# Making the low part of every fourth weight chunk with ScalarE and an adding DMA instead of VectorE

## The chip, the cores and the metric

The kernel runs on one core of one Trainium2 chip. The metric is the device time of one execution in microseconds (us). PE is TensorE, DVE is VectorE, ACT is ScalarE, POOL is GpSimd and SP is SyncE, whose queue issues most transfers.

## The reference, cut to what matters

Two layers work on 512 rows of width 2048. Each one norms its rows, projects them, mixes them, projects again and adds the normed result to its input:

```python
def even_mixer(h, w_in, pool_w, pool_scale, w_out, cos, sin):
    z = h @ w_in
    a_in, a_gate, q, k, v, b_gate = jnp.split(z, _split_points(EVEN_COLS), axis=-1)
    ya = causal_pool_mixer(a_in, pool_w, pool_scale) * jax.nn.silu(a_gate)
    yb = dilated_attention(q, k, v, cos, sin) * jax.nn.silu(b_gate)
    return jnp.concatenate([ya, yb], axis=-1) @ w_out
...
    for i in range(DEPTH):
        if i % 2 == 0:
            h = rmsnorm(x, e_pre_norm[j])
            y = even_mixer(h, e_w_in[j], e_pool_w[j], e_pool_scale[j], e_w_out[j], cos, sin)
            x = x + rmsnorm(y, e_post_norm[j])
        else:
            h = rmsnorm(x, o_pre_norm[j])
            y = odd_mixer(h, o_w_in[j], o_sgu_norm_g[j], o_sgu_norm_b[j], o_sgu_w[j], o_sgu_b[j],
                          o_conv_w[j], o_conv_b[j], o_conv_norm_g[j], o_conv_norm_b[j], o_w_out[j])
            x = x + rmsnorm(y, o_post_norm[j])
```

The odd layer's mixer has the same two projections around a gating unit and a convolution of width 31. All data are float32.

## The kernel before, in words

All large weights are cut into 402 chunks of 128 x 1024 float32 (512 KB), which are used in one fixed order, numbered 0 to 401. A float32 product is made of three products of a narrower type (float32r): weight and activation are both split into a high part (the value rounded) and a low part (the rest), and PE adds low x high, high x low and high x high. The activations' parts stand in the buffers `Ah` and `Al`. The weights' parts are made while the program runs, by `Weights.split`: SP loads the raw chunk into a `wraw` buffer (L54), ACT writes the rounded copy `whi` (L64), and DVE subtracts it from the raw chunk to give `wlo` (L65). There are three buffers each for `wraw`, `whi` and `wlo`, so the parts of chunk i go where those of chunk i-3 were, and ACT can start on chunk i when PE has ended chunk i-3. A raw buffer is free for its next load when both the parts have been made from it.

PE uses a chunk in one of two ways. `zt_item` (L137 to L139) and `nat_item` with four row tiles (L162 to L164) issue 24 matmuls on each chunk; stages of these are called full-width here. `nat_item` with two row tiles issues 12 on each chunk; these are columns 2 and 3 of each output projection (`out_projection`, 32 chunks in each layer) and the odd layer's `owv` projection (32 chunks). They are called half-width stages here: chunks 210 to 273 and 370 to 401, 96 chunks. In a half-width stage the matmuls on one chunk begin with one or two that take `whi` (L162), and the first that takes `wlo` (L163) comes right after them.

The instructions' order on each engine is set at build time by a scheduler, which estimates times of its own; each engine then runs its own list in that order, and waits on semaphores. POOL does little: small scalar steps of the norms (`rsqrt_of`, L114 and L116), the reductions over partitions of the attention and the convolution, and some stores. At the end of each half of an output projection, `boundary` adds the normed rows to x, stores them with a DMA issued by POOL (L328) and has PE transpose them (L222).

Of the kernel before, what the change touches and what calls it, by code (L numbers as in the profile page):

```python
# [13 lines left out]
F32 = mybir.dt.float32  # L14
FR = mybir.dt.float32r
AF = mybir.ActivationFunctionType
OP = mybir.AluOpType
# [18 lines left out]


class Weights:
    """Streams the weight chunks in the order of use and splits each into two float32r parts."""

    def __init__(self, nc, raw_pool, split_pool, chunks, raw_bufs, ahead):
        self.nc, self.raw_pool, self.split_pool, self.chunks = nc, raw_pool, split_pool, chunks
# [14 lines left out]
    def split(self, upto):  # L57
        while len(self.parts) < min(upto, len(self.chunks)):
            i = len(self.parts)
            self.load(i + 1)  # L60
            hi = self.split_pool.tile([P, 1024], FR, tag="whi", name=f"whi{i}")
            lo = self.split_pool.tile([P, 1024], FR, tag="wlo", name=f"wlo{i}")
            for c in ((slice(0, 512), slice(512, 1024)) if i == 0 else (slice(0, 1024),)):
                self.nc.scalar.activation(hi[:, c], self.raw[i][:, c], AF.Copy)  # L64
                self.nc.vector.tensor_tensor(lo[:, c], self.raw[i][:, c], hi[:, c].bitcast(F32), op=OP.subtract)  # L65
            self.parts.append((hi, lo))

# [9 lines left out]
def trunk(ctx: ExitStack, tc: tile.TileContext, x, xt, out, ewv, ewz, ewo, epw, epost,  # L77
# [38 lines left out]
        nc.gpsimd.tensor_tensor(r, v, neghalf, op=OP.pow)  # L116
        return r

# [1 line left out]
    items = []  # L120

    def add_item(chunks, pe, after=None):
# [88 lines left out]
        items.clear()  # L211
        return pos

# [1 line left out]
    def to_A(half, pcol0):  # L215
        rows = [yrow(2 * half), yrow(2 * half + 1)]
        for kq in range(8):
            ps = sbank(f"tr{half}_{kq}").rearrange("p (k t) -> p k t", k=2)
            for j in range(2):
                k = 2 * kq + j  # L220
                for t in range(2):
                    nc.tensor.transpose(ps[:, j, P * t:P * t + P], rows[t][:, P * k:P * k + P], ident)  # L222
            for j in range(2):
                k = 2 * kq + j
                g = pc[:, pcol0 + k:pcol0 + k + 1]
                ah = Ah[:, k, 256 * half:256 * half + 256]
                nc.scalar.activation(ah, ps[:, j, :], AF.Copy, scale=g)
                nc.vector.scalar_tensor_tensor(Al[:, k, 256 * half:256 * half + 256], ps[:, j, :], g,
                                               ah.bitcast(F32), op0=OP.mult, op1=OP.subtract)
            if kq % 2 == 1:  # L230
                yield 1

    post = {}

# [1 line left out]
    first = {}  # L236

    def first_loads(i, t, chunk):
# [94 lines left out]
            yield 1  # L333
        yield from to_A(half, P_OPRE)

# [1 line left out]
    def split_y(ks):  # L337
        for k in ks:
            nc.scalar.activation(Ah[:, k, :], Y[:, k, :], AF.Copy)
            nc.vector.tensor_tensor(Al[:, k, :], Y[:, k, :], Ah[:, k, :].bitcast(F32), op=OP.subtract)  # L340
# [37 lines left out]
                nat_item(wo, c, [2 * half, 2 * half + 1], evac(c), order=order,  # L378
                         stagger=layer == 1 and half == 1 and c == 3)

    # ================= start =================
    nc.gpsimd.memset(neghalf, -0.5)
    cones = cpool.tile([P, 1], F32, name="cones")
    nc.gpsimd.memset(cones, 1.0)
# [2 lines left out]
    for key in ("ssq", "v", "r"):  # L387
        first[key] = small.tile([P, 4], F32, name=f"first_{key}", bufs=1)

    # ================= even layer, attention =================  # L390
    att_stack = ExitStack()
    att = att_stack.enter_context(tc.tile_pool(name="att", bufs=1))
    V1 = att.tile([P, 4, S], F32, name="V1")
# [120 lines left out]
    chunk_list = []  # L514
    w = Weights(nc, raw_pool, split_pool, chunk_list, 3, 2)

    # The whole program's chunks are listed first, so that loads and splits run ahead of their use.
    program = []

    def section(build):  # L520
# [18 lines left out]

    section(build_attention)  # L540

    # ================= even layer, pooling =================
    mix = {}

    pooled = {}
# [66 lines left out]
    section(build_pooling)  # L612
    section(lambda: out_projection(ewo, 0, (4, 5, 6, 7, 0, 1, 2, 3)))

    # ================= odd layer =================
    od = {}

    def ov_after(c):
# [144 lines left out]
    section(build_odd)  # L763
    section(lambda: out_projection(owo, 1, range(8)))

    # ================= emission =================
    w.first_loads = first_loads
    w.load(3)
    start(norm_first())
# [111 lines left out]
def build(arrays):  # L881
    nc = bacc.Bacc("TRN2", target_bir_lowering=False, num_devices=1)
    args = {}
    for name, a in arrays.items():
        args[name] = nc.dram_tensor(f"in_{name}_dram", a.shape, mybir.dt.from_np(a.dtype), kind="ExternalInput").ap()
    args["out"] = nc.dram_tensor("out_0_dram", (S, D), F32, kind="ExternalOutput").ap()
    with tile.TileContext(nc, schedule_with_timeline_sim=True) as tc:
        trunk(tc, **args)
    return nc
# [7 lines left out]
```

## Time and profile before

| | |
|---|---|
| median of the timed runs | 2072.81 us (2 runs, 2072.59 to 2073.03) |
| profiled execution, span from first to last instruction | 2071.4 us |
| busy: PE / DVE / ACT / POOL | 2055.5 / 1156.7 / 647.1 / 87.4 us |
| mean granted TensorE clock | 0.999 |

The span is 1.4 us under the median of the timed runs. Busy time is the time in which an engine had an instruction in work; matmuls are pipelined, so two of them may overlap in the rows, and their starts tell more than their ends. "Idle before" of an instruction is the time in which its engine had nothing in work ahead of it, with what ended that time behind the arrow.

### The profile page before, as it was taken

To read this page: it belongs to the slowest core of one execution; us is meant where nothing else is said; L and a number is where in the kernel's file an instruction comes from. 1 tells how busy PE (TensorE), PEld (TensorE's weight loads), DVE (VectorE), ACT (ScalarE), POOL (GpSimd) and SP (SyncE) were. 2 spreads that over 40 slices of the span, in tenths; PEclk is the share of its full clock that TensorE was granted. 3 is DMA by queue.
4 is the path that set the end of the run, shared out by engine and by line. 5 is a ranking of instruction groups with operands and counts; after the bars stand their busy time and mean duration, and the time that the engine had idled before them with its cause. 6 is when DMAs were issued, how large, how long until landed. Compare 5 with 4: busy or idle time off the path is not lost.

```text
span 2071.4 us, 22339 instructions
## 1 busy us (share of the span) xinstructions
PE 2055.5 (99%) x9064; PEld 1699.7 (82%) x9064; DVE 1156.7 (56%) x1385; ACT 647.1 (31%) x793; POOL 87.4 (4%) x86
## 2 busy tenths in 40 slices
PE   8999999999999999999999999999999999999998
PEld 8988888889988888888888888888888888888886
DVE  4725656555224656566542435775889996324255
ACT  6422222323222322223332324553122223323243
POOL 1000101000000101001000000100000001000002
PEclk9999999999999999999999999999999999999999
DMA  8332222232322222222223337864222222223465
GB/s 299 92 101 89 94 83 82 86 98 82 92 92 92 89 85 91 82 92 82 92 93 101 112 97 222 281 216 155 87 92 92 97 97 92 92 91 122 133 211 196
DMA packets 68472, 241.78 MB, mean 117 GB/s; under 512 B 7792, under 2 KB 8048, under 8 KB 67088
## 3 DMA queue, kind: packets, MB, share of 16 engines
q1 hardware_dynamic: 67152, 234.05, 35.0%
q0 software_dynamic: 1216, 6.29, 0.8%
q8 instruction: 71, 1.16, 0.2%
q14 instruction: 33, 0.27, 0.0%
HBM read 231.93 MB, written 8.39 MB: 116 GB/s over the span
## 4 chain that ended last, share of the span: by engine, by line
PE 97%; DMA 1%; DVE 1%; ACT 0%; issue 0%; POOL 0%; SPq 0%; DVEq 0%; ACTq 0%; POOLq 0%
PE z L138 20%; PE z L137 20%; PE z L139 20%; PE n L162 11%; PE n L163 11%; PE n L164 11%; PE sg L457 1%; DMA wraw<-in_owv_dram 0%; DVE Y L313 0%; PE ob L497 0%; PE ob L496 0%; PE oa L490 0%; PE sgu L640 0%; PE sa L445 0%; PE tr L222 0%; DMA wraw<-in_owo_dram 0%
## 5 line engine op out<-in xcount | busy, mean ns | idle before, releaser
L65 DVE TENSOR_TENSOR wlo<-wraw,whi 128x1024 fp32r<-128x1024 f32 (+1 forms) x403 | 504.1, 1251 | 571.3 <-ACT whi L64 570.6
L137 PE MATMUL z<-Ah,wlo 128*128 128x512 f32 x1792 | 710.5, 396 | 0.0
L138 PE MATMUL z<-Al,whi 128*128 128x512 f32 x1792 | 708.8, 396 | 0.0
L64 ACT ACTIVATE whi<-wraw 128x1024 fp32r<-128x1024 f32 (+1 forms) x403 | 425.5, 1056 | 906.9 <-PE z L139 463.8
L139 PE MATMUL z<-Ah,whi 128*128 128x512 f32 x1792 | 708.7, 395 | 0.0
L163 PE MATMUL n<-wlo,Ah 128*128 128x512 f32 x1024 | 406.8, 397 | 0.3 <-DVE wlo L65 0.2
L164 PE MATMUL n<-whi,Ah 128*128 128x512 f32 x1024 | 405.5, 397 | 0.0
L139 PEld LDWEIGHTS z<-Ah,whi 128*128 128x128 f32 x1792 | 336.6, 188 | 81.0
L137 PEld LDWEIGHTS z<-Ah,wlo 128*128 128x128 f32 x1792 | 336.7, 188 | 80.6
L138 PEld LDWEIGHTS z<-Al,whi 128*128 128x128 f32 x1792 | 336.7, 188 | 80.6
L162 PE MATMUL n<-whi,Al 128*128 128x512 f32 x1024 | 392.3, 398 | 6.7 <-DVE Al L263 6.7
L162 PEld LDWEIGHTS n<-whi,Al 128*128 128x128 f32 x1024 | 223.2, 218 | 41.6 <-DVE Al L263 6.7
L163 PEld LDWEIGHTS n<-wlo,Ah 128*128 128x128 f32 x1024 | 223.4, 218 | 36.3 <-DVE wlo L65 1.3
L164 PEld LDWEIGHTS n<-whi,Ah 128*128 128x128 f32 x1024 | 223.3, 218 | 35.0
L681 DVE SCALAR_TENSOR_TENSOR Y<-dp,pc,Y 128x512 f32<-128x512 f32 x240 | 174.3, 749 | 3.6
L423 DVE LOAD_MASK_SELECT sw<-qk x32 | 0.4, 14 | 125.4 <-ACT qk L422 125.4
L422 ACT ACTIVATE qk<-z 128x512 f32<-128x512 f32 x32 | 19.1, 597 | 145.3 <-PE z L139 145.3
L474 POOL PARTITION_ALL_REDUCE mw<-mv x8 | 14.3, 1784 | 798.9 <-DVE mv L472 798.9
L424 DVE TENSOR_TENSOR sw<-sw,rp 32x512 f32<-32x512 f32 x32 | 34.3, 1071 | 1.1
L425 DVE TENSOR_TENSOR qk<-qk,rp 32x512 f32<-32x512 f32 x32 | 34.0, 1063 | 0.0
L426 DVE TENSOR_TENSOR qk<-qk,sw 32x512 f32<-32x512 f32 x48 | 32.3, 673 | 0.2
L735 DVE TENSOR_TENSOR Y<-Y,og 128x512 f32<-128x512 f32 x16 | 11.1, 691 | 38.0 <-ACT og L734 38.0
(153 smaller groups left out, 908.1 us busy)
## 6 DMA issues: line engine op xcount, KB each, us to landing
wraw<-in_ewz_dram SPq DMA_DIRECT2D x144, 512.0 KB, 3.7
wraw<-in_owz_dram SPq DMA_DIRECT2D x80, 512.0 KB, 3.8
wraw<-in_ewo_dram SPq DMA_DIRECT2D x48, 512.0 KB, 4.2
wraw<-in_owo_dram SPq DMA_DIRECT2D x48, 512.0 KB, 3.9
wraw<-in_ewv_dram SPq DMA_DIRECT2D x47, 512.0 KB, 3.6
wraw<-in_owv_dram SPq DMA_DIRECT2D x32, 512.0 KB, 3.8
xn<-in_x_dram SPq DMA_DIRECT2D x4, 1024.0 KB, 8.7
xr<-in_x_dram SPq DMA_DIRECT2D x16, 256.0 KB, 5.1
```

Of the source, the lines that this page charges most:

```text
L64: self.nc.scalar.activation(hi[:, c], self.raw[i][:, c], AF.Copy)
L65: self.nc.vector.tensor_tensor(lo[:, c], self.raw[i][:, c], hi[:, c].bitcast(F32), op=OP.subtract)
L137: nc.tensor.matmul(ps, wl[:, j], Ah[:, k, :], start=first, stop=False)
L138: nc.tensor.matmul(ps, wh[:, j], Al[:, k, :], start=False, stop=False)
L139: nc.tensor.matmul(ps, wh[:, j], Ah[:, k, :], start=False, stop=last)
L162: nc.tensor.matmul(ps, tok(Al, k, t), wh[:, j], start=first, stop=False)
L163: nc.tensor.matmul(ps, tok(Ah, k, t), wl[:, j], start=False, stop=False)
L164: state["mm"] = nc.tensor.matmul(ps, tok(Ah, k, t), wh[:, j], start=False, stop=last).ins
L424: nc.vector.tensor_tensor(perm_out(sw), perm_out(sw), perm_in(sin), op=OP.mult)
L425: nc.vector.tensor_tensor(perm_out(t[0:32, :]), perm_out(t[0:32, :]), perm_in(cos), op=OP.mult)
L426: nc.vector.tensor_tensor(t[0:32, :], t[0:32, :], sw, op=OP.add)
L681: nc.vector.scalar_tensor_tensor(acc, dp[:, k:k + S], wk, acc, op0=OP.mult, op1=OP.add)
```

## The change

From chunk 16 on, every chunk whose number leaves 3 when divided by 4 (19, 23, ..., 399: 96 chunks) gets its low part in another way. ACT writes the rounded copy `whi` as before, and a second time the same copy with its sign turned into `wlo`. Then a DMA issued by POOL adds the raw chunk onto `wlo` where it stands. DVE has no part in these chunks. Of the 96, 24 lie in half-width stages (211, 215, ..., 271 and 371, 375, ..., 399). Behind L66 the lines of the changed kernel are numbered higher by 4, and `wlo` is negated in L66 and added to in L67. Comments that the change also takes out do nothing.

```diff
             for c in ((slice(0, 512), slice(512, 1024)) if i == 0 else (slice(0, 1024),)):
                 self.nc.scalar.activation(hi[:, c], self.raw[i][:, c], AF.Copy)
+                if i >= 16 and i % 4 == 3:
+                    self.nc.scalar.activation(lo, self.raw[i], AF.Copy, scale=-1.0)
+                    self.nc.gpsimd.dma_start(lo.bitcast(F32), self.raw[i], accum_op=OP.add)
+                    continue
                 self.nc.vector.tensor_tensor(lo[:, c], self.raw[i][:, c], hi[:, c].bitcast(F32), op=OP.subtract)
```

The scheduler orders the lists anew. In the rows below the number behind `whi`, `wlo` and `wraw` is that of the chunk; what follows the next underscore only tells buffers apart. On ACT, around chunk 219 in the first half-width stage (`junk0` is the squaring of an output column), the order before is

```order
L64 ACTIVATE whi217_7835<-wraw217_7781 128x1024
L64 ACTIVATE whi218_7854<-wraw218_7800 128x1024
L64 ACTIVATE whi219_7873<-wraw219_7820 128x1024
L64 ACTIVATE whi220_7895<-wraw220_7839 128x1024
L349 ACTIVATE junk0_6022,sq0_0_98<-n_210_0_7743 128x512
```

and in the changed kernel, at the same place of the same engine:

```order
L64 ACTIVATE whi217_7885<-wraw217_7830 128x1024
L64 ACTIVATE whi218_7904<-wraw218_7850 128x1024
L66 ACTIVATE wlo219_7924<-wraw219_7870 128x1024
L64 ACTIVATE whi219_7923<-wraw219_7870 128x1024
L353 ACTIVATE junk0_6058,sq0_0_98<-n_210_0_7792 128x512
L64 ACTIVATE whi220_7946<-wraw220_7889 128x1024
```

The negated copy comes ahead of the high part, so that the DMA's input is made first. At chunk 235 it is the other way round:

```order
L64 ACTIVATE whi235_8339<-wraw235_8268 128x1024
L66 ACTIVATE wlo235_8340<-wraw235_8268 128x1024
```

On POOL, the first boundary of the even layer has these rows before (`x1d` is the store of a row tile, `v_z` and `r_z` the scale of the next norm):

```order
L328 DMA x1d_85<-xr0_0_7735 128x2048
L114 TENSOR_SCALAR v_z0_8061<-ssz0_8059 128x1
L116 TENSOR_TENSOR r_z0_8063<-v_z0_8061,neghalf_84 128x1
L328 DMA x1d_85<-xr0_1_7814 128x2048
L114 TENSOR_SCALAR v_z1_8092<-ssz1_8090 128x1
L116 TENSOR_TENSOR r_z1_8094<-v_z1_8092,neghalf_84 128x1
```

and in the changed kernel these, up to the second boundary, with the adding DMAs (L67) among them:

```order
L332 DMA x1d_85<-xr0_1_7864 128x2048
L67 DMA wlo231_8226<-wraw231_8125 128x1024
L118 TENSOR_SCALAR v_z1_8145<-ssz1_8143 128x1
L120 TENSOR_TENSOR r_z1_8147<-v_z1_8145,neghalf_84 128x1
L67 DMA wlo235_8340<-wraw235_8268 128x1024
...
L332 DMA x1d_85<-xr0_3_8262 128x2048
L118 TENSOR_SCALAR v_z3_8578<-ssz3_8576 128x1
L120 TENSOR_TENSOR r_z3_8580<-v_z3_8578,neghalf_84 128x1
L67 DMA wlo247_8656<-wraw247_8558 128x1024
```

Chunk 231's DMA stands behind the store of a row tile, and chunk 247's behind the last step of the second boundary.

## Rows read from the trace of the kernel before

**Rows 1.** The page: busy time of the engines, and the chain that ended last.

```profile
PE 2055.5 (99%) x9064; PEld 1699.7 (82%) x9064; DVE 1156.7 (56%) x1385; ACT 647.1 (31%) x793; POOL 87.4 (4%) x86
...
PE 97%; DMA 1%; DVE 1%; ACT 0%; issue 0%; POOL 0%; SPq 0%; DVEq 0%; ACTq 0%; POOLq 0%
```

**Rows 2.** Waits of PE in the span: us in total, times, longest.

```profile
PE n L162 <- DVE Al L263: 6.7, 1, 6.7
PE n L163 <- DVE wlo L65: 0.2, 1, 0.2
```

**Rows 3.** The page's groups: busy, mean ns of one, idle before.

```profile
L65 DVE TENSOR_TENSOR wlo<-wraw,whi 128x1024 fp32r<-128x1024 f32 (+1 forms) x403 | 504.1, 1251 | 571.3 <-ACT whi L64 570.6
...
L64 ACT ACTIVATE whi<-wraw 128x1024 fp32r<-128x1024 f32 (+1 forms) x403 | 425.5, 1056 | 906.9 <-PE z L139 463.8
```

**Rows 4.** Timeline, full-width stage: chunk 28's last matmul, chunk 31's high part and first matmul.

```profile
171.52 0.40 PE L139 MATMUL z<-Ah,whi 128*128 128x512 f32 x1
...
171.95 1.06 ACT L64 ACTIVATE whi<-wraw 128x1024 fp32r<-128x1024 f32 x1 [4.05 <-PE z L139]
...
182.96 0.40 PE L137 MATMUL z<-Ah,wlo 128*128 128x512 f32 x1
```

**Rows 5.** Timeline, half-width stage: the same for chunk 219, with its low part.

```profile
1259.32 0.40 PE L164 MATMUL n<-whi,Ah 128*128 128x512 f32 x1
...
1259.75 1.06 ACT L64 ACTIVATE whi<-wraw 128x1024 fp32r<-128x1024 f32 x1 [1.74 <-PE n L164]
...
1260.85 1.23 DVE L65 TENSOR_TENSOR wlo<-wraw,whi 128x1024 fp32r<-128x1024 f32 x1 [1.57 <-ACT whi L64]
...
1265.62 0.39 PE L163 MATMUL n<-wlo,Ah 128*128 128x512 f32 x1
```

**Rows 6.** DMA issues of POOL: the first store of 2022 us alone, the four L328.

```profile
out_dram<-Y POOLq DMA_DIRECT2D x1, 256.0 KB, 3.3
...
x1d<-xr POOLq DMA_DIRECT2D x4, 1024.0 KB, 7.6
...
DMA to landing us min/median/max: 7.5/7.6/9.6
```

**Rows 7.** Raw chunks' loads, us to landing: 300 to 400 us, then 1220 to 1290 us.

```profile
wraw<-in_ewz_dram SPq DMA_DIRECT2D x17, 512.0 KB, 3.7
...
wraw<-in_ewo_dram SPq DMA_DIRECT2D x21, 512.0 KB, 4.4
```

**Rows 8.** Windows: a half-width and a full-width stage; the last columns are clock, DMA share, GB/s.

```profile
1223.00:1430.00 207.00, 206.74 (x928) 166.96 (x927) 128.66 (x141) 102.36 (x140) 18.43 (x29) 1.00 0.68 217
1430.00:1961.00 531.00, 531.00 (x2306) 428.67 (x2305) 350.92 (x448) 138.59 (x168) 10.48 (x12) 1.00 0.31 99
```

**Rows 9.** Timeline of the two boundaries: POOL's last steps, and ACT and PE for chunks 231, 235, 247.

```profile
1295.89 1.48 POOL L328 DMA_DIRECT2D x1d<-xr  x1
...
1299.57 0.48 PE L163 MATMUL n<-wlo,Ah 128*128 128x512 f32 x1
...
1310.43 1.06 ACT L64 ACTIVATE whi<-wraw 128x1024 fp32r<-128x1024 f32 x1 [0.92 <-PE tr L222]
...
1313.91 0.40 PE L163 MATMUL n<-wlo,Ah 128*128 128x512 f32 x1
...
1348.35 0.48 PE L163 MATMUL n<-wlo,Ah 128*128 128x512 f32 x1
...
1349.03 0.56 POOL L116 TENSOR_TENSOR r_z<-v_z,neghalf 128x1 f32<-128x1 f32 x1
```

**Rows 10.** Timeline of PE's first matmuls.

```profile
8.57 0.63 PE L163 MATMUL n<-wlo,Ah 128*128 128x512 f32 x1
9.00 0.63 PE L164 MATMUL n<-whi,Ah 128*128 128x512 f32 x1
...
9.74 0.40 PE L163 MATMUL n<-wlo,Ah 128*128 128x512 f32 x1
9.98 0.40 PE L164 MATMUL n<-whi,Ah 128*128 128x512 f32 x1
```

## Prediction

> **What bounds the kernel now.** First the page's busy times and its chain: PE is busy in 99% of the span and the chain that ended last is PE for 97% [rows 1]. Then the waits of PE: in 2071.4 us it stood still for a low part made by DVE once, for 0.2 us, and for 6.7 us at the very start, where no changed chunk is [rows 2]. So the bound is PE's own list of matmuls. Nothing that only unloads DVE can give back more than 0.2 us, and the question is whether a changed chunk's low part now arrives too late for PE. For that the timeline is read at one chunk in each kind of stage, from the moment at which ACT may start on it to the first matmul that takes its low part.
>
> In a full-width stage ACT starts on chunk 31 at 171.95 us, 0.43 us after the start of the last matmul on chunk 28, and PE takes its low part first at 182.96: 11.01 us [rows 4]. In a half-width stage it is 1259.75 to 1265.62 for chunk 219: 5.87 us [rows 5]. Both follow from the three buffers: two chunks of PE work lie between. Between the two PE starts of 1259.32 and 1265.62 lie 27 matmuls, so one is 0.233 us and a half-width chunk of 12 is 2.80 us. Before the change ACT and DVE need 2.33 us of the 5.87 (to 1262.08), so 3.5 us are spare there and some 8.7 us in a full-width stage.
>
> **Removed.** 96 subtractions of 1.25 us [rows 3]: 120 us of DVE's 1156.7. DVE is waited for 0.2 us, so this is worth nothing on the path.
>
> **Added on ACT.** 96 negated copies. They have the shape and the function of the high part's copy, so 1.06 us each [rows 3], 101 us on top of 647.1; ACT still idles for more than half of the span. As the order shows, the negated copy usually comes first and the high part 1.06 us later, with 3 us or more left to its first matmul. Worth nothing by itself; 1.06 us of it stands in the new chain.
>
> **Added: 96 DMAs from POOL, and PE's wait for them.** The chain for a changed chunk is now copy (1.06 us), the DMA's issue, its landing, PE. A handover between engines costs 0.04 us (ACT ends at 1260.81, DVE starts at 1260.85 [rows 5]). What is left for a DMA from issue to landing, without a stall, is 5.87 - 1.06 - 2 x 0.04 = 4.73 us in a half-width stage and 11.01 - 1.14 = 9.87 us in a full-width one.
>
> The trace has no adding DMA, so its time is bounded by neighbours. Below: the load of the same 512 KB by SP lands in 3.7 us where little else moves [rows 7]. Above: 9.6 us, the slowest 1 MB store of POOL [rows 6]. Between them, POOL's 256 KB store took 3.3 us and its 1 MB stores 7.6 us [rows 6]. Were this a plain copy of 512 KB, the line through the two would give 3.3 + (7.6 - 3.3) / 3 = 4.73 us. But an addition needs both operands, so 1 MB is read, and as a 1 MB transfer it would take 7.6 us; half of the bytes are written, though. I take the mean, 6.17 us. That half-width stages are crowded speaks for the upper half: the DMA engines are busy 68% there against 31% in a full-width stage [rows 8], and a raw chunk lands in 4.4 us instead of 3.7 [rows 7].
>
> The sum, with 6.17 us:
> - Full-width stages, 72 chunks: 9.87 us are available, so nothing. What hides the DMA is the two chunks of PE work ahead of it; past 9.87 us each microsecond more costs 72.
> - Half-width stages, 24 chunks. Two (211 and 371) are split while PE still has a full-width chunk before them, and cost nothing. Three stand at the boundaries and come apart. The other 19 stall PE for 6.17 - 4.73 = 1.44 us each: 27.4 us.
> - Chunk 231: in POOL's list its DMA is behind the row tile's store, whose issue ended at 1295.89 + 1.48 = 1297.37 [rows 9]. Landing at 1303.54, wanted at 1299.57: 3.97 us. The last norm scale (`r_z1`) is now queued behind this DMA's issue, and PE's transposes (L222) wait for it; the one issue in these rows took 1.48 us, which lies inside the stall.
> - Chunk 235: ACT starts at 1310.43, makes the high part first, and ends the negated copy 2.12 us later. With two handovers and 6.17 us the sum lands at 1318.80, wanted at 1313.91: 4.89 us.
> - Chunk 247: its DMA is behind `r_z3`, which ended at 1349.03 + 0.56 = 1349.59; landing at 1355.76, wanted at 1348.35 [rows 9]: 7.41 us.
>
> Together 27.4 + 4.0 + 4.9 + 7.4 = 43.7 us.
>
> **The raw buffer** is held until the DMA has landed, 7.27 us after ACT's start instead of 2.33, and SP's queue, which issues in order, holds the loads behind it back. With a load of 4.4 us the next chunk in that buffer is there at 11.7 us. If that is chunk i+3, ACT would have begun on it at 3 x 2.80 + 1.44 = 9.84 us, so it is 1.8 us late, and the 3.5 us spare of a DVE-made chunk cover that. If it is i+4, the next changed one, ACT wants it at 12.64 us. So nothing; if loads grow by 1.5 us because the additions crowd the DMA engines, about 0.6 us on each of some 20 chunks, 12 us, which stays in the range.
>
> The profiled execution would so become 2071.4 + 43.7 = 2115.1 us, and with the 1.4 us between span and median **2117 us**, 2.1% over 2072.8. About 2% (41 us) is what a measurement of this kernel can tell from no change; the forecast crosses that at a DMA of 6.07 us, so it is close.
>
> **Rivals.** (1) The DMA fits: it lands within 4.7 us in half-width stages. For it speaks the 3.7 us load and the line through POOL's stores; against it the second operand and the crowded stages. Then the 19 regular chunks cost nothing, and the three at the boundaries, which are late through order and not through the transfer, cost 2.5 + 3.5 + 6.0 = 12 us at 4.73 us and 9 us at 3.7: 2073 to 2090 us, not slower. Beside this: the Trainium skill (DMA: Bandwidth & Descriptors, section Anatomy of one DMA — SWDGE (gpsimd) path) gives such a DMA about 2.0 us and its bytes at 436 GB/s, an estimated 3.2 us here; and (Collectives: The Full Stack, section The bandwidth ceiling: the fold count and why AG ≠ RS ≠ AR) says that an add in a DMA reads two sources and runs at half the rate, which makes an estimated 4.4 us. By both, this rival would win. The trace's stores took longer than that rule has it (3.3 us where it gives 2.6, 7.6 where it gives 4.4), which is why the chance stays low.
>
> (2) The addition is much slower than a copy of 1 MB, and full-width stages stall as well. At 11 us: 19 x 6.27 + 31 at the boundaries + 72 x 1.13 = 231 us, 2304 us. Nothing in the trace shows it, nothing excludes it. Between 8 and 9.87 us only the half-width part grows, to 2157 to 2198 us.
>
> (3) PE's clock falls in the stalls. The clock was granted in full (1.00) in the windows shown [rows 8], but there PE hardly ever stood. At the program's start, after the 6.7 us wait, matmuls begin 0.43 us apart, later 0.24 us [rows 10]: 1.2 and then 2.4 GHz. Some 7 matmuls were slow. If each of 22 stalls did that, 22 x 7 x 0.2 = 31 us more: 2148 us.
>
> (4) The freed DVE shows: 0.2 us. Not measurable.
>
> **How the numbers follow.** Forecast (DMA of 5 to 8 us, 2090 to 2157): 0.58. Fits: 0.20. Between 8 and 9.87 us: 0.06. Full-width too: 0.10. Clock: 0.05. Faster: 0.01. About a third of the forecast's chance and all of rival 1 lie within 2%: 0.41. The rest is slower: 0.58. The range leaves out the low third of rival 1 and the case of full-width stalls, and reaches to the bound of 9.6 us: 19 x 4.87 + 26 = 119 us. So 2078 to 2190 us.
>
> **What would show it.** PE's waits should list L167 of the changed kernel behind a DMA on `wlo`, some 22 times, 1 to 2 us mostly, only in 1230 to 1430 us and after 1970 us; L137 (L141 now) should not appear. POOL's L67 should land in about 6 us in these stretches. In full-width stages matmuls should follow each other as before. No wait of PE on `wlo` at all proves rival 1; waits in zt stages prove rival 2; a granted clock under 1.00 there proves rival 3. The forecast is wrong most easily in the one number that no row shows, the landing of the adding DMA: each microsecond of it is worth 22 us.

## The result, and the profile after

| | before | after |
|---|---|---|
| median of the timed runs | 2072.81 us | 2133.61 us (2132.92 to 2134.31) |
| span of the profiled execution | 2071.4 us | 2132.5 us |
| ratio, 95% interval | | 1.0291 (1.0274 to 1.0309) |

The kernel became 60.8 us slower. The page of the changed kernel answers to [rows 1]: PE's busy time has grown by 19.9 us for the same 9064 matmuls, and DMA has 7% of the chain that ended last, where it had 1%.

```profile
PE 2075.4 (97%) x9064; PEld 1710.0 (80%) x9064; DVE 1038.0 (49%) x1289; ACT 736.7 (35%) x889; POOL 170.5 (8%) x182
...
PE 89%; DMA 7%; issue 2%; DVE 1%; ACT 1%; POOL 1%; SPq 0%; DVEq 0%; ACTq 0%; POOLq 0%
```

PE's waits in the whole span (us in total, times, longest) answer to [rows 2]:

```profile
PE n L167 <- DMA wlo<-wraw: 25.4, 15, 3.7
PE n L166 <- DVE Al L267: 6.9, 1, 6.9
PE n L166 <- ACT whi L64: 4.0, 1, 4.0
PE n L167 <- DVE wlo L69: 3.3, 3, 2.0
PE tr L226 <- DVE Y L336: 2.1, 1, 2.1
PE z L141 <- DVE wlo L69: 1.9, 1, 1.9
PE tr L226 <- issue: 1.5, 1, 1.5
```

The 6.9 us at the start answer to the 6.7 and 0.2 us of before. New are 25.4 us behind the adding DMAs, and 12.8 us in seven waits behind other work. So the 61.1 us by which the span grew come apart as 25.4 + 12.8, the 19.9 us more of PE's busy time, and 3.0 us of idle time outside these waits (57.1 us between span and busy time less the waits' 45.1, against 15.9 - 6.9 before). These 3.0 us lie at the program's end: from the end of PE's last matmul to the end of the span it was 8.9 us before and is 11.9 us now. POOL's closing instructions stand there (L887 before, L891 now):

```profile
L887 POOLq DRAIN  x3: 46/102/2839, 2065.2 to 2071.2; - x3
...
L891 POOLq DRAIN  x3: 46/102/8432, 2123.3 to 2132.3; - x3
```

The first and longest of the three took 2.84 us before and ended 2.1 us ahead of the last store's landing; it takes 8.43 us now and ends 3.6 us behind that landing. In the experiments below it took 2.84 us where no adding DMA was issued (3), 4.80 with 24 of them (2), 6.47 with 72 (1), and 8.19 with 93 (8 and 10).

The new instructions, in the page's groups, as long as [rows 3] had them for the copy:

```profile
L67 POOL DMA_DIRECT2D wlo<-wraw x96 | 84.1, 876 | 1554.3 <-ACT wlo L66 1520.7
...
L66 ACT ACTIVATE wlo<-wraw 128x1024 fp32r<-128x1024 f32 x96 | 101.7, 1059 | 301.4 <-PE z L141 207.2
```

How long an adding DMA takes from issue to landing, by stretch: first 0 to 1223 us, which is full-width, then 1223 to 1460 us, which is half-width but for its ends.

```profile
DMA to landing us min/median/max: 4.5/4.6/5.6
...
DMA to landing us min/median/max: 4.5/5.3/10.0
```

The windows, with the columns of [rows 8]: a half-width stretch, a full-width one (its first 30 us or so are still half-width here), and then a short one, right behind PE's wait that ended at 1271.34 us.

```profile
1223.00:1430.00 207.00, 183.90 (x780) 144.99 (x779) 95.30 (x111) 101.35 (x138) 29.25 (x41) 0.96 0.75 223
1430.00:1961.00 531.00, 528.10 (x2288) 425.78 (x2287) 331.96 (x429) 165.28 (x192) 31.02 (x37) 1.00 0.44 125
...
1271.40:1274.80 3.40, 3.40 (x8) 2.72 (x9) 0.00 (x0) 0.00 (x0) 0.00 (x0) 0.50 0.82 266
```

In the half-width stretch PE is busy for 184 of 207 us (before: all of it) and the granted clock is 0.96 (before: 1.00). The last row shows where the 0.04 are: right behind the wait PE runs 8 matmuls in 3.40 us at a clock of 0.50, which is 1.2 GHz, with nothing to wait for. There are eight such stretches ahead of the end, and this is the sum of their windows:

```profile
sum 30.71, PE 29.16 PEld 23.22 DVE 10.11 ACT 9.61 POOL 2.18; mean PE 3.65 PEld 2.90 DVE 1.26 ACT 1.20 POOL 0.27
```

A matmul begins every 0.425 us there and every 0.233 us elsewhere, so some 13 of the 29.16 us are the clock's (an estimate from these figures). The other 7 of the 19.9 us come with the stops themselves, as far as the rows tell: a matmul lasts 0.40 us and the next begins 0.233 us after it, so each of the 21 more stops leaves 0.16 us of the last matmul in the busy time (3.5 us), and the first matmul behind a stop is longer (0.50 us at 1256.43 below).

The timeline around chunk 219, for which [rows 5] showed the kernel before. SPq is SP's issue of a transfer.

```profile
1249.45 1.06 ACT L66 ACTIVATE wlo<-wraw 128x1024 fp32r<-128x1024 f32 x1 [1.51 <-PE n L167]
...
1250.81 0.86 POOL L67 DMA_DIRECT2D wlo<-wraw  x1 [13.14 <-ACT wlo L66]
...
1256.43 0.50 PE L167 MATMUL n<-wlo,Ah 128*128 128x512 f32 x1 [0.72 <-DMA wlo<-wraw]
...
1256.75 0.33 SPq L54 DMA_DIRECT2D wraw<-in_ewo_dram  x1
1257.66 0.49 SPq L54 DMA_DIRECT2D wraw<-in_ewo_dram  x1
1258.71 0.43 SPq L54 DMA_DIRECT2D wraw<-in_ewo_dram  x1
1260.56 1.06 ACT L64 ACTIVATE whi<-wraw 128x1024 fp32r<-128x1024 f32 x1 [4.21 <-DMA wraw<-in_ewo_dram]
1261.20 0.40 PE L167 MATMUL n<-wlo,Ah 128*128 128x512 f32 x1
...
1263.57 1.06 ACT L66 ACTIVATE wlo<-wraw 128x1024 fp32r<-128x1024 f32 x1 [1.94 <-PE n L168]
1264.92 0.86 POOL L67 DMA_DIRECT2D wlo<-wraw  x1 [13.25 <-ACT wlo L66]
1271.34 0.79 PE L167 MATMUL n<-wlo,Ah 128*128 128x512 f32 x1 [3.45 <-DMA wlo<-wraw]
```

Read from the top: chunk 215's adding DMA, issued at 1250.81, landed at 1256.39, and only then could SP issue the load of chunk 218, which goes into the same raw buffer. The loads of 219 and 220 stood behind it in SP's order, so three loads went out within 2 us, with loads of `xr` between them. They took 3.7, 5.8 and 7.6 us. PE's last matmul that takes chunk 216's low part began at 1261.20. The next negated copy may follow such a start by 0.43 us (chunk 215's did: 1249.02 to 1249.45), so ACT could have begun on chunk 219 at 1261.63; its raw chunk landed at 1263.46 and ACT began at 1263.57, 1.94 us late. (The list names a PE instruction as what ended ACT's wait, but the wait covers several semaphores; the load is the one that landed 0.1 us before.) The adding DMA then ran beside the loads behind it and took 6.4 us instead of 4.6. The 1.94 us of the late load and the 1.65 us of landing over the 4.73 us at hand make 3.59 us, against 3.45 us of PE's wait.

In the full-width stage, the timeline of chunk 31, as in [rows 4]:

```profile
172.62 1.06 ACT L66 ACTIVATE wlo<-wraw 128x1024 fp32r<-128x1024 f32 x1 [3.59 <-PE z L141]
...
173.98 0.85 POOL L67 DMA_DIRECT2D wlo<-wraw  x1 [21.55 <-ACT wlo L66]
...
184.09 0.40 PE L141 MATMUL z<-Ah,wlo 128*128 128x512 f32 x1
```

The DMA took 4.6 us and landed at 178.59, 5.5 us before PE wanted the chunk.

At the boundaries, the timeline that answers to [rows 9]: first chunk 231, then the place of chunk 247.

```profile
1307.03 1.48 POOL L332 DMA_DIRECT2D x1d<-xr  x1
...
1308.50 0.95 POOL L67 DMA_DIRECT2D wlo<-wraw  x1
...
1318.59 0.50 PE L167 MATMUL n<-wlo,Ah 128*128 128x512 f32 x1 [3.40 <-DMA wlo<-wraw]
...
1372.73 1.06 ACT L64 ACTIVATE whi<-wraw 128x1024 fp32r<-128x1024 f32 x1 [6.58 <-DMA wraw<-in_owv_dram]
...
1373.84 1.22 PE L166 MATMUL n<-whi,Al 128*128 128x512 f32 x2 [3.98 <-ACT whi L64]
```

Chunk 231's DMA stood behind the store and took 10.0 us beside its 1 MB and the loads of raw chunks and of `xr` that SP issued meanwhile. Chunk 247's DMA made nobody wait, because PE had already stood for 4.0 us behind chunk 246's high part, whose raw chunk came late.

### The profile page after: what moved, and what is told of

Its sections match the earlier page's. It is cut to its first block, busy times and chain, and to the rows that moved or that the text cites. A ratio compares the mean times of both kernels' runs of the same rounds, so it can differ in the third digit from the quotient of the medians.

```text
span 2132.5 us, 22656 instructions
## 1 busy us (share of the span) xinstructions
PE 2075.4 (97%) x9064; PEld 1710.0 (80%) x9064; DVE 1038.0 (49%) x1289; ACT 736.7 (35%) x889; POOL 170.5 (8%) x182
## 4 chain that ended last, share of the span: by engine, by line
PE 89%; DMA 7%; issue 2%; DVE 1%; ACT 1%; POOL 1%; SPq 0%; DVEq 0%; ACTq 0%; POOLq 0%
PE z L141 19%; PE z L142 19%; PE z L143 19%; PE n L167 9%; PE n L168 9%; PE n L166 9%; DMA wlo<-wraw 4%; DMA wraw<-in_owv_dram 1%; PE sg L461 1%; DMA wraw<-in_ewo_dram 1%; ACT wlo L66 1%; PE ob L501 0%; PE ob L500 0%; PE oa L494 0%; PE sa L449 0%
## 5 line engine op out<-in xcount | busy, mean ns | idle before, releaser
L69 DVE TENSOR_TENSOR wlo<-wraw,whi 128x1024 fp32r<-128x1024 f32 (+1 forms) x307 | 375.6, 1224 | 524.3 <-ACT whi L64 524.1
L167 PE MATMUL n<-wlo,Ah 128*128 128x512 f32 x1024 | 414.3, 405 | 28.8 <-DMA wlo<-wraw 25.4
L168 PE MATMUL n<-whi,Ah 128*128 128x512 f32 x1024 | 410.0, 401 | 0.0
L166 PE MATMUL n<-whi,Al 128*128 128x512 f32 x1024 | 396.9, 401 | 10.9 <-DVE Al L267 6.9
L67 POOL DMA_DIRECT2D wlo<-wraw x96 | 84.1, 876 | 1554.3 <-ACT wlo L66 1520.7
L66 ACT ACTIVATE wlo<-wraw 128x1024 fp32r<-128x1024 f32 x96 | 101.7, 1059 | 301.4 <-PE z L141 207.2
L356 DVE TENSOR_TENSOR Y<-n,gpost 128x512 f32<-128x512 f32 x32 | 22.1, 691 | 37.5 <-PE n L168 37.5
```

What stands on the lines that cost most here:

```text
L66: self.nc.scalar.activation(lo, self.raw[i], AF.Copy, scale=-1.0)
L67: self.nc.gpsimd.dma_start(lo.bitcast(F32), self.raw[i], accum_op=OP.add)
L166: nc.tensor.matmul(ps, tok(Al, k, t), wh[:, j], start=first, stop=False)
L167: nc.tensor.matmul(ps, tok(Ah, k, t), wl[:, j], start=False, stop=False)
L168: state["mm"] = nc.tensor.matmul(ps, tok(Ah, k, t), wh[:, j], start=False, stop=last).ins
```

## The experiments

The theory after the result: the adding DMA itself is no longer than PE's lead where it runs alone, and the loss sits in the half-width stages in three shares that feed each other: the adding DMA beside loads and behind other work on POOL, raw chunks that come late because the DMA holds their buffers, and TensorE's clock after the waits. Its rivals were that the 96 DMAs cost something everywhere, that ACT's copies or the new order of the lists are what costs, and that a longer lead alone would mend it. Times are given as the median and its distance from the kernel before on the same chip (the changed kernel: +60.8 us).

**1. Only the 72 full-width chunks changed.**

```diff
-                if i >= 16 and i % 4 == 3:
+                if i >= 16 and i % 4 == 3 and not (210 <= i < 274 or i >= 370):
```

> The change is made in the 72 chunks of the full-width stages alone; the 24 of the half-width stages get their low part from VectorE as before. Theory (the loss is PE waiting for late low parts in the half-width stages, and the clock that falls after long waits there): 2073 to 2077 us, granted clock 0.999, PE's waits on the adding DMA 0 to 2 us. Rival A (the added transfers slow whatever runs beside them): the loss goes with the number of DMAs, 72/96 of 61 us, about 2118 us.

2078.18 us, +4.7, 1.2 us over what was expected; ratio 1.0023 (1.0014 to 1.0032). PE's waits, apart from the one at the start and 0.4 us on one low part of DVE:

```profile
PE z L141 <- DVE wlo L69: 1.8, 1, 1.8
```

No adding DMA makes PE wait here. Of the 4.2 us by which the profiled span grew, 1.8 are this wait, 1.6 are PE's busy time (a stretch at 0.50 stands behind the wait), and 1.1 the longer end of the program, while the wait at the start is 0.3 us shorter. Three quarters of the DMAs cost under a tenth of the loss.

**2. Only the 24 half-width chunks changed.**

```diff
-                if i >= 16 and i % 4 == 3:
+                if i >= 16 and i % 4 == 3 and (210 <= i < 274 or i >= 370):
```

> The change is made in the 24 chunks of the half-width stages alone. Theory: nearly the whole loss, 2128 to 2136 us, with the clock at 0.96 in the half-width windows. Rival A: 24/96 of the loss, about 2088 us.

2127.58 us, +54.1, 0.4 us under what was expected; ratio 1.0261 (1.0246 to 1.0276).

```profile
PE n L167 <- DMA wlo<-wraw: 25.0, 14, 3.7
```

The waits behind the DMA are those of the whole change, and 54.1 + 4.7 = 58.8 of its 60.8 us are found in the two parts. The loss is the half-width stages'.

**3. ACT's negated copy stays, and DVE adds the raw chunk instead of the DMA.**

```diff
-                    self.nc.gpsimd.dma_start(lo.bitcast(F32), self.raw[i], accum_op=OP.add)
+                    self.nc.vector.tensor_tensor(lo, self.raw[i], lo.bitcast(F32), op=OP.add)
```

> All 96 chunks get the negated copy from ScalarE, but VectorE adds the raw chunk onto it and no DMA is issued. Theory: the chain is as long as before (a copy of 1.06 us and an addition of 1.25 us), so 2072 to 2076 us. Rival B (ScalarE's 101 us more push its other work, and with it PE, back): 2085 us or more.

2076.68 us, +3.2, 0.7 us over what was expected; ratio 1.0015 (1.0006 to 1.0025). ACT's 96 copies, with the order of the lists that the scheduler made for this version, cost 3 us; behind the start PE waits 1.7 us for a boundary's norm and 0.5 and 0.4 us for low parts. The other 57.6 us come with the DMA in the adding step's place, the order made for it included.

**4. Eight matmuls that nobody reads, ahead of the first low-part matmul of every changed half-width chunk,** so that PE is busy where it would stand.

```diff
+                if ti == 0 and j == 0 and len(tts) == 2 and len(done) % 4 == 3:
+                    dummy = sbank(f"fill{len(done)}")
+                    for n in range(8):
+                        nc.tensor.matmul(dummy, tok(Al, k, t), wh[:, j], start=n == 0, stop=n == 7)
```

> The changed kernel with 8 extra matmuls (1.87 us) on each changed chunk of the half-width stages, before the first one that takes the low part; their result goes to a PSUM bank that nothing reads. They add 24 x 1.87 = 45 us of PE work. Theory (the clock falls because PE stands still, and costs some 15 to 20 us): PE is busy in most of the waits, the granted clock in the half-width windows rises from 0.96 to 0.99 or more, and in spite of the added work the time is 2110 to 2130 us. Rival C (the clock falls for another reason): clock as before, 2145 to 2160 us.

2151.70 us, +78.3; ratio 1.0378 (1.0361 to 1.0395). The 2110 to 2130 us were missed, and the time lies in the rival's range, 2145 to 2160 us. Its windows of the half-width stretches, the odd layer's last, are these (the changed kernel had a clock of 0.96 in both):

```profile
1223.00:1460.00 237.00, 221.27 (x949) 177.11 (x949) 102.89 (x117) 109.19 (x146) 36.42 (x42) 0.96 0.69 207
1990.00:2118.00 128.00, 123.31 (x528) 98.48 (x527) 42.90 (x45) 48.70 (x61) 13.89 (x20) 1.00 0.69 203
```

The edit was too blunt: 24 x 8 x 0.233 = 44.8 us of work went in, and at nine of the 24 chunks there was no wait to fill. The clock came back in the second window and not in the first, so this run leaves the clock's share open; experiment 9 repeats it where the waits are.

**5. The DMA copies the raw chunk onto `wlo` instead of adding it.** The subtraction of the high part is thereby left out in the 96 chunks; the run tells only times.

```diff
-                    self.nc.gpsimd.dma_start(lo.bitcast(F32), self.raw[i], accum_op=OP.add)
+                    self.nc.gpsimd.dma_start(lo.bitcast(F32), self.raw[i])
```

> The DMA copies the raw chunk over the low part instead of adding it (the subtraction of the high part is left out in these 96 chunks); all else is as in the changed kernel. Theory D (the second operand makes the transfer long): it lands about 1 us sooner than the adding one (3.5 us instead of 4.6 in full-width stages), and the time is 2085 to 2110 us. Theory E (issue and completion make it long, the sum is nearly free): 4.3 to 4.6 us and 2128 to 2136 us.

2108.23 us, +34.7; ratio 1.0169 (1.0154 to 1.0184). L67's landing over the whole span, and PE's wait for it:

```profile
DMA to landing us min/median/max: 2.8/2.9/6.6
...
PE n L167 <- DMA wlo<-wraw: 7.4, 5, 2.5
```

The addition makes the same transfer 1.7 us longer (4.6 against 2.9 us), and its issue on POOL 0.86 us instead of 0.53. With the short transfer 18 of the 25.4 us of waiting go, and more than half of the loss stays. Of its 34.7 us 5.3 lie at the program's end, where POOL's last step took 10.7 us. The rest fits a DMA that still holds a raw buffer and still crowds other transfers, but this run does not take these shares apart.

**6. Four raw buffers instead of three** (the room comes from one `qk` buffer less, and from `osb` placed over masks no longer used).

```diff
-    raw_pool = ctx.enter_context(tc.tile_pool(name="raw_pool", bufs=3))
+    raw_pool = ctx.enter_context(tc.tile_pool(name="raw_pool", bufs=4))
...
-    w = Weights(nc, raw_pool, split_pool, chunk_list, 3, 2)
+    w = Weights(nc, raw_pool, split_pool, chunk_list, 4, 2)
```

> The changed kernel with four raw buffers instead of three (room is made by 7 instead of 8 buffers for rotated queries and keys and by putting one constant of the odd layer over masks that are no longer used). If the raw buffer that is held until the DMA lands makes loads late, and so part of the waits: PE's waits in the half-width stages fall by a third or more and the time is 2105 to 2122 us. If it costs nothing, as the prediction had it: 2129 to 2135 us.

2124.07 us, +50.6; ratio 1.0249 (1.0233 to 1.0264). It lies between the two ranges that were expected, 2105 to 2122 and 2129 to 2135 us. ACT's waits for raw chunks in 1223 to 1460 us, first of the kernel before, then of the changed kernel:

```profile
ACT whi L64 <- DMA wraw<-in_ewo_dram: 10.0, 6, 3.3
ACT whi L64 <- DMA wraw<-in_owv_dram: 4.9, 2, 3.9
...
ACT whi L64 <- DMA wraw<-in_owv_dram: 24.7, 7, 6.6
...
ACT whi L64 <- DMA wraw<-in_ewo_dram: 12.7, 7, 4.2
```

and then of this one, where the `in_ewo_dram` wait is off the list:

```profile
ACT whi L64 <- DMA wraw<-in_owv_dram: 5.8, 2, 5.7
```

The change took these waits from 14.9 to 37.4 us; the fourth buffer takes them to 5.8, and the kernel gained 10.2 us. That is a share, and not the whole: PE still waited 20.2 us, 14 times, behind the adding DMA, and chunk 219's now took 9.4 us beside loads of raw chunks and of `xr`. (The profiled execution was the longest of its four, 2128.8 us against 2123.2 to 2124.4.)

**7. Four buffers for `wlo`,** so that a changed chunk's low part may be started one chunk earlier (the room as in 6).

```diff
-            lo = self.split_pool.tile([P, 1024], FR, tag="wlo", name=f"wlo{i}")
+            lo = self.split_pool.tile([P, 1024], FR, tag="wlo", name=f"wlo{i}", bufs=4)
...
-    w = Weights(nc, raw_pool, split_pool, chunk_list, 3, 2)
+    w = Weights(nc, raw_pool, split_pool, chunk_list, 3, 3)
```

> The changed kernel with four buffers for the low part and the splits issued one chunk earlier (room as with four raw buffers), so that the DMA may start up to 1.7 us sooner in a half-width stage. Theory (lateness against PE is the whole matter): most waits on the DMA go, but for those behind other POOL work; 2080 to 2100 us. Rival (crowded DMA engines and late loads keep it): 2115 us or more.

2136.77 us, +63.3, far over the 2080 to 2100 us expected; ratio 1.0301 (1.0284 to 1.0318). So a longer lead alone does not mend it.

```profile
DMA to landing us min/median/max: 4.6/6.2/9.4
...
PE n L167 <- DMA wlo<-wraw: 31.7, 17, 3.9
```

Started earlier, the adding DMA ran beside a raw chunk's load (chunk 223's went out at 1277.95 us, a load at 1278.00): 6.2 us instead of 4.6 over the whole span. The lead was spent on that.

**8. Chunks 231, 247 and 391 left to DVE,** whose DMAs stand behind stores or norm steps on POOL.

```diff
-                if i >= 16 and i % 4 == 3:
+                if i >= 16 and i % 4 == 3 and i not in (231, 247, 391):
```

> The changed kernel, but chunks 231, 247 and 391, whose DMA stands behind stores or norm steps in GpSimd's list, get their low part from VectorE. Theory (order on GpSimd's queue costs there): 10 to 18 us less than the changed kernel, 2115 to 2123 us. If the order does not matter: 3 of 24 chunks' share, 5 to 7 us less.

2122.13 us, +48.6; ratio 1.0236 (1.0221 to 1.0251). Three chunks of 96 are worth 12.2 us, a fifth of the loss, where 5 to 7 us were expected if the order on POOL did not matter. The wait behind chunk 246's late raw chunk stays, at 4.3 us, so that one is not the order's.

**9. Fourteen matmuls that nobody reads, at five chunks with a long wait** (as in 4, with 14 for 8).

```diff
+                if ti == 0 and j == 0 and len(done) in (219, 231, 259, 379, 391):
```

> As the changed kernel, but at five of the chunks on which PE waited longest or long (219, 231, 259, 379, 391) 14 matmuls that nobody reads (14 x 0.233 = 3.3 us) stand before the first matmul that takes the low part; 16.3 us of work in all, at places where PE waited 2 to 3.7 us. Theory C (part of the 61 us is TensorE's clock, which falls to its lower level right after the long waits): no wait of PE on a low part's DMA and no stretch at 1.2 GHz is left at these five places, and the work costs little: 2122 to 2132 us, at or under the changed kernel's 2133.6. Rival (the clock falls for other reasons, or the waits move to the next changed chunk): stretches at 1.2 GHz remain as many, and the time is 2136 us or more.

2131.5 us, +57.9; ratio 1.0286 (1.0268 to 1.0303). Windows around chunks 219, 259, 379 and 391, of the changed kernel:

```profile
1255.00:1278.00 23.00, 18.83 (x74) 14.51 (x73) 7.51 (x7) 8.45 (x11) 0.86 (x1) 0.93 0.75 232
1408.00:1424.00 16.00, 13.65 (x53) 10.64 (x52) 10.39 (x13) 7.10 (x8) 2.69 (x5) 0.89 0.71 219
2034.00:2052.00 18.00, 14.44 (x51) 11.16 (x50) 5.90 (x6) 6.89 (x10) 0.86 (x1) 0.81 0.76 237
2078.00:2094.00 16.00, 12.27 (x47) 9.44 (x46) 6.84 (x8) 3.49 (x4) 4.14 (x7) 0.89 0.87 280
```

and around the same chunks with the fills:

```profile
1254.00:1277.00 23.00, 21.93 (x94) 17.04 (x93) 7.51 (x7) 9.61 (x13) 0.86 (x1) 1.00 0.76 235
1406.00:1422.00 16.00, 16.00 (x70) 12.86 (x69) 11.37 (x14) 7.22 (x8) 3.65 (x5) 1.00 0.76 245
2026.00:2050.00 24.00, 24.00 (x104) 19.28 (x105) 6.67 (x7) 10.24 (x13) 1.72 (x2) 1.00 0.85 256
2076.00:2098.00 22.00, 21.17 (x91) 16.71 (x90) 9.61 (x11) 8.59 (x12) 3.42 (x6) 1.00 0.84 246
```

The clock is whole at all four, and PE took in 70 more matmuls (16.3 us of work at full speed) while its busy time rose by 9.2 us only, from 2075.4 to 2084.6. The time, at the upper end of what was expected, stood at +57.9 against +60.8. So the work was free, and at these four places the clock fell because PE stood, not for the place in the program. Two details missed. At chunk 231 2.15 us of the wait were left, and waits at chunks without a fill (375, 387) grew to 2.2 and 3.0 us. And three stretches at 0.50 are left elsewhere, with waits of 2.1, 4.3 and 3.0 us.

**10. Four raw buffers, and the three chunks of 8 left to DVE.**

> Four raw buffers, and chunks 231, 247 and 391 left to VectorE. If the raw buffer's hold and the order on POOL's queue are separate shares, their gains of 9.5 and 11.5 us add: 2109 to 2117 us, with PE's waits on the low part's DMA some 14 us, what the landing alone costs. Rival (both act through the same late loads, so that one gain contains the other): 2119 us or more.

2112.29 us, +38.7, as expected; ratio 1.0187 (1.0172 to 1.0203). The gains of 6 and 8 add: 60.8 - 10.2 - 12.2 = 38.4.

```profile
PE n L167 <- DMA wlo<-wraw: 15.6, 13, 3.9
```

What is left of the waits behind the DMA is the adding DMA beside loads, which neither edit takes away: the longest wait, 3.9 us, stood behind one that took 8.8 us next to loads of raw chunks and of `xr`. No version tried is faster than the kernel before.

## Why the prediction was right, and where its sum was not

The direction and the mechanism held: PE waits for the adding DMA in half-width stages and nowhere else, 15 times where some 22 were forecast, and the time lies in the range. The forecast of 2117 us was 17 us short, and the sum behind it was made of one term too large (43.7 us of waits, where 25.4 were measured) and 35.7 us left out: 12.8 of other waits, 19.9 of busy time and 3.0 at the end. That the two errors offset each other is luck.

- **PE is the bound, and a freed DVE is worth nothing:** right. DVE lost 119 us of work and no time came back.
- **ACT's copies at nothing:** 3 us, with the order of the lists that came with them (experiment 3).
- **Full-width stages at nothing:** right as to the DMA, which lands with 5.5 us to spare. Most of the 4.7 us of experiment 1 are one wait of 1.8 us, behind a reduction on POOL and its followers on ACT, which was not followed further, and the slow matmuls behind it.
- **4.73 us at hand in a half-width stage:** right. Chunks 215, 227, 243 and 255 landed in 5.58, 5.87, 5.73 and 5.67 us and cost PE 0.72, 1.00, 0.86 and 0.81 us, each some 0.13 us under the difference. But two errors cancel in the 4.73: POOL issued 0.3 us after ACT's end, not 0.04 (1249.45 + 1.06 to 1250.81), and the negated copy needs only the old low part's buffer, which PE frees 0.23 us before the old high part's.
- **A landing of 6.17 us for every chunk:** wrong as one number. Eleven of the 24 landed in 5.0 us or less and cost PE 1.6 us together; eleven took 5.4 to 6.4 us, and 391 and 231, behind and beside stores, 7.8 and 10.0. Ten of the first eleven (all but 247) ran beside other transfers of the program for 2.2 us or less, summed over the transfers, and the second eleven for 2.8 us or more. DVE's work alone does not stretch it: in full-width stages it landed in 4.5 us with DVE idle (issued at 440.30) and with DVE busy nearly throughout (1506.91). The 19 chunks that the sum took as regular made PE wait 20.8 us instead of 27.4, of which 3.7 are 391's, which was an edge and wasn't counted as one. The Trainium skill (DMA: Bandwidth & Descriptors, section Anatomy of one DMA — SWDGE (gpsimd) path) gave an estimated 3.2 us for a copy, and with the half rate that it states for the add of a ReduceScatter (Collectives: The Full Stack, section The bandwidth ceiling: the fold count and why AG ≠ RS ≠ AR) an estimated 4.4 us; the traces have medians of 2.9 and 4.6 us where little else moves, so that rule was nearer than the mean that was taken from stores. The stores that spoke against it were no measure of a DMA alone: the one of 3.3 us, issued at 2022.16, ran beside a raw chunk's load issued at 2019.80 that landed at 2024.26. Neither estimate covers what the transfer takes beside loads, which decided here against rival 1.
- **The boundaries:** 231 3.4 us (3.97 forecast), 235 1.2 (4.89), 247 none (7.41). All waits behind the DMA make 25.4 us, against 43.7. That 231 comes out near is luck: its DMA took 10.0 us and not 6.17, but PE was late as well and wanted the low part 6.7 us after the store's issue, not 2.2. 235's landed in 4.55 us, which is 1.6 of the 3.65 us by which its wait fell short of the forecast; for the rest PE was late already, as it was for 247, by the next point.
- **The raw buffer at nothing:** the step that failed. It looked at one buffer and asked whether its next load comes in time. But SP issues in order: the held load keeps back the loads behind it, they go out together when the DMA has landed, and crowd each other and the next adding DMA, as chunk 219 shows. A fourth raw buffer gave 10 us back (experiment 6).
- **The clock as a rival of 0.05:** wrong in kind. It was counted as another outcome of 31 us, and it came with the forecast: 19.9 us more of busy time, of which some 13 are the clock's. It did not take every stop, as the 31 us had it, but eight of 22. Whoever forecasts 40 us of waits in this program has to add it to the sum.
- **The end of the program:** in no term. POOL's closing step is 5.6 us longer and 3.0 us of it show (the result's section).
- **2% as the least that can be told from no change:** too wide. The interval of experiment 1, at +4.7 us, runs from 1.0014 to 1.0032.

That 25.4 + 12.8 + 19.9 + 3.0 give the span's 61.1 us is no test, since span is busy time and idle time. How the 12.8 us part between late loads, order and slow matmuls ahead is argued from the timeline, and not shown wait by wait.

## What to carry to other kernels

An operation moved from an engine to a DMA is costed at four places: its landing beside the traffic of that stage (not alone), the buffers that it holds until it lands and the loads queued behind them, what stands ahead of it on the issuing queue, and the program's end. Look first for the stage with the shortest lead: 24 of 96 chunks made nine tenths of this loss. And where PE is the bound, a wait costs more than its length, since the matmuls behind a long one can run slower.

## What the runs showed of the hardware

- A DMA of 512 KB that adds within SBUF landed in 4.5 us at the least and 4.6 in the median where little else moved (0 to 1223 us), a copying one in 2.8 and 2.9 (whole span); issues took 0.86 and 0.53 us of POOL.
- Beside loads in half-width stages the adding one took 5.4 to 6.4 us, with four raw buffers up to 9.4, and beside a 1 MB store and loads 10.0.
- POOL's closing step took 2.84 us with no adding DMA issued by POOL, 4.80 with 24, 6.47 with 72, 8.19 with 93, 8.43 with 96, and 10.68 with 96 copying ones.
- In the changed kernel eight of PE's waits behind the start, of 1.9 to 4.0 us, were followed by a stretch at a granted clock of 0.50 (1.2 GHz), which in three of them began while PE still stood; one of 2.0 us and all those of 1.5 us and less were not.
